# TensorE's instructions held in the order in which a two-layer hybrid backbone kernel gives them out

## The chip, the cores and the metric

The kernel runs on one core of a Trainium2 chip. The metric is device time in microseconds (us) of one execution. The chip's engines named here are TensorE (PE in the profile, with PEld for its weight loads), VectorE (DVE), ScalarE (ACT), GpSimd (POOL) and SyncE (SP, which here issues most of the DMAs).

## The reference, cut to what matters

Two post-norm layers run over 1024 latent tokens and 256 context tokens of width 1024, all in float32. In each layer the normalised input is modulated by vectors that come from a small product with `w_ada`, goes through one input projection, then through three branches (windowed attention, a gated depthwise convolution with LayerNorm, and a bidirectional linear recurrence), and the gated branches are merged and projected back.

```python
for l in range(DEPTH):                                    # DEPTH = 2, D_MODEL = 1024
    shift, scale, gate = jnp.split(jax.nn.silu(c) @ w_ada[l] + b_ada[l], 3, axis=-1)
    ...
    h = layer_norm(x) * (1.0 + scale[:, None]) + shift[:, None]
    hc = layer_norm(ctx) * (1.0 + scale_c) + shift_c
    q, k, v, g_att, u_conv, g_conv, x_lru, g_lru = split_in_proj(h @ w_in[l])
    ...
    y_att = window_attention(q, k, v, kc, vc, attn_sink[l])
    y_conv = conformer_conv(u_conv, ...)
    y_lru = hf_l + hb_l                                   # two rglru_direction scans
    out = merge_branches(h, (y_att, y_conv, y_lru), (g_att, g_conv, g_lru), ...)   # also uses sigmoid(h @ w_gate)
    x_new = deepnorm_post(x, gate[:, None] * out, ln_g[l], ln_b[l])
    # the context tokens go the same way, but not in the last layer
```

## The kernel before, in words

Every large product is made of float32r matmuls: the left and the right factor are each cut into a high part (`hi`) and a rest (`lo`), and hi·hi, hi·lo and lo·hi are added up in PSUM. So a weight arrives by DMA as `raw`, ACT copies it to `whi`, and DVE subtracts to get `wlo` (class `Wt`, method `load`; the tags `whi` and `wlo` have four buffers each, `NW = 4`). The activations stand transposed in SBUF as `hchi`/`hclo` (context, 256 columns) and `hlhi`/`hllo` (latent, two tiles of 512 columns).

The order of the work is made twice. First the Python code gives instructions out in an order of its own. In `phase1` (projections, branches, gates) and `phase2` (merge and output) a `Driver` runs generators, called streams here: recurrence, attention scores, attention values, convolution, gates and others. A stream yields between pieces of its work, and the Driver picks the next piece by its own estimate of when each engine is free (`LEAD`, `SLACK`, `MARGIN`, `PRIO`). PE, ACT and DVE are reached through a `Meter`, which adds up these estimates, so that nearly every one of their instructions has line 73 in the profile. Second, the tile framework is opened with `schedule_with_timeline_sim=True`: its scheduler takes the instructions of all engines with their dependencies and orders each engine's list anew by a simulation of its own. What runs is this second order.

Four places matter below. `emit_h0` is the start: it loads the input, normalises it, transposes it on PE (`p0` tiles in PSUM, 80 transposes), and ACT (`hf0`, then a copy) and DVE make the hi and lo parts. `ada_pair` is called 16 times between the gate projections of a layer: it loads two `w_ada` pieces, runs 16 matmuls with `csr` into one PSUM tile and calls `ada_fin`, where ACT copies the row (`arow`) and two small matmuls with `sel` follow; there is no yield in it and no wait for the weights' readiness:

```python
        for k in range(KD):
            for v in range(2):
                pe.matmul(out=ps[0:4, 0:256], lhsT=csr[:, k, :], rhs=ws[k // 4][v][:, k % 4, :],
                          start=(k == 0 and v == 0), stop=(k == KD - 1 and v == 1))
        ada_fin(l, [jj, jj + 1], ps, 4, row)
```

`att_values` transposes the softmax rows `P` into a PSUM tile `pt`, ACT makes `ph` and DVE makes `pl` from it, and the matmuls into `yp` follow; between the transposes and these matmuls the stream yields. `norm` in `phase2` normalises the finished rows `xp`, transposes them (eight transposes into one of the two `ps2` buffers) and ACT modulates them (`hf`), which gives the next layer its `hl`/`hc` tiles.

Of the kernel before, what the change touches and what calls it, by code (L numbers as in the profile page):

```python
# [51 lines left out]
class Meter:  # L52


    def __init__(self, eng, cost):
        self.eng, self.cost, self.t = eng, cost, 0.0

    def __getattr__(self, name):
        f = getattr(self.eng, name)
        if name.startswith("dma"):  # L60
            return f

        def call(*a, **k):
            out = k.get("out", a[0] if a else None)
            src = k.get("in_", out) if name in ("reduce_max", "bn_stats") else out
            n = 1
            for v in src.shape[1:]:
                n *= v
            if len(a) == 2 and name == "tensor_copy":
                k = dict(k, in_=a[1])  # L70
                a = a[:1]
            self.t += self.cost(name, n, k)
            return f(*a, **k)  # L73

        return call

# [113 lines left out]
def kernel(  # L190
# [5 lines left out]
):  # L196
    nc = tc.nc
    pool, sp = nc.gpsimd, nc.sync
    pe, act, dve = Meter(nc.tensor, pe_cost), Meter(nc.scalar, act_cost), Meter(nc.vector, dve_cost)
    drv_ = Driver(pe, act, dve)  # L200

    K = ctx.enter_context(tc.tile_pool(name="const", bufs=1))
# [118 lines left out]
    class Wt:  # L321


        def __init__(self, src, a, b, home=None):
            self.own = home is None
            if self.own:
                wlive[0] += 1
            self.ap, self.ready = drv_.side(lambda: self.load(src, a, b, home or W))
# [1135 lines left out]
```

## Time and profile before

| | |
|---|---|
| median of 3 runs | 2307.94 us (2307.21 to 2312.17) |
| profiled execution | 2307.8 us, of which the span of instructions is 2306.0 us |
| mean clock granted to TensorE | 0.990 of full speed |
| busy share of the span | PE 98%, PEld 81%, DVE 73%, ACT 44%, POOL 4% |

The page gives each engine's busy time; the windows view gives it for a stretch, with the granted clock in the column PEclk. In the timeline a row is a run of like instructions with its start and length; matmuls overlap, so the distance between two starts, not the length of a row, is what a matmul costs in a dense stretch. An idle time ahead of an instruction stands in brackets, with the instruction whose end released it.

### The profile page before, as it was taken

The numbers are of one execution on the slowest core, as the hardware profiler recorded it, in microseconds if no ns is written. First come the engines' busy times: TensorE is split into PE (matmuls) and PEld (weight loads), VectorE is DVE, ScalarE is ACT, GpSimd is POOL, SyncE is SP. The second block draws the span as 40 slices with busy tenths as digits, with TensorE's granted clock in tenths as the row PEclk, the third lists the DMA queues.
The fourth block names the chain that finished last, engine by engine and source line by source line (L and its number), as shares of the span: only waits on it lengthen the run. The fifth ranks groups of instructions, "written<-read, shape, count | busy, mean of one in ns | idle before, by whom it ended". The sixth has DMA issues, their size and how long they took to land.

```text
span 2306.0 us, 29961 instructions
## 1 busy us (share of the span) xinstructions
PE 2249.3 (98%) x11344; PEld 1871.8 (81%) x11344; DVE 1678.9 (73%) x2453; ACT 1003.4 (44%) x1642; POOL 86.7 (4%) x140
## 2 busy tenths in 40 slices
PE   7999999999999999999999999999999999999998
PEld 2888888888888887888888788888888878778886
DVE  5579967868959875545678749869778787655667
ACT  4555563245444575422122644565344456542110
POOL 1000000000000111000001100000000011000002
PEclk8999999999999999999999999999999999999999
DMA  7223323433334232655562222233423334347532
GB/s 276 76 73 101 115 73 126 142 112 108 108 101 138 80 117 87 203 167 168 151 206 74 94 66 67 80 92 128 142 90 97 89 122 131 111 136 227 160 128 92
DMA packets 270946, 279.90 MB, mean 121 GB/s; under 512 B 19769, under 2 KB 199889, under 8 KB 270801
## 3 DMA queue, kind: packets, MB, share of 16 engines
q1 hardware_dynamic: 242288, 226.06, 31.4%
q10 hardware_dynamic: 28512, 51.92, 6.4%
q8 instruction: 89, 1.46, 0.3%
q14 instruction: 57, 0.46, 0.1%
HBM read 203.04 MB, written 74.88 MB: 121 GB/s over the span
## 4 chain that ended last, share of the span: by engine, by line
PE 88%; DVE 5%; ACT 2%; DMA 2%; issue 2%; SPq 0%; POOLq 0%; POOL 0%; ACTq 0%; DVEq 0%
PE ps L73 82%; PE yp L73 3%; PE pt L73 2%; PE pa L73 1%; DVE acc L73 1%; DMA raw<-in_w_ada_dram 1%; DVE P L73 1%; DVE pl L73 1%; DVE wlo L73 1%; DMA yst<-yd 1%; ACT whi L73 0%; DMA qd<-qd 0%; DVE xp L73 0%; PE p L73 0%; ACT hf L73 0%
## 5 line engine op out<-in xcount | busy, mean ns | idle before, releaser
L73 PE MATMUL ps<-hlhi,whi 128*128 128x512 f32 x1728 | 681.9, 395 | 2.2 <-DVE gs L73 1.0
L73 PE MATMUL ps<-hllo,whi 128*128 128x512 f32 x1728 | 678.4, 393 | 0.0
L73 PE MATMUL ps<-hlhi,wlo 128*128 128x512 f32 x1728 | 676.8, 392 | 0.0
L73 PEld LDWEIGHTS ps<-hlhi,wlo 128*128 128x128 f32 x1728 | 325.8, 189 | 67.5 <-issue 0.4
L73 PEld LDWEIGHTS ps<-hlhi,whi 128*128 128x128 f32 x1728 | 326.5, 189 | 66.5 <-DVE pl L73 2.2
L73 PEld LDWEIGHTS ps<-hllo,whi 128*128 128x128 f32 x1728 | 326.2, 189 | 62.7 <-issue 0.7
L73 DVE SCALAR_TENSOR_TENSOR acc<-u,cwt,acc 128x1296 f32<-128x1296 f32 (+1 forms) x240 | 342.3, 1426 | 2.2
L73 ACT ACTIVATE whi<-raw 128x1024 fp32r<-128x1024 f32 x180 | 190.0, 1058 | 334.1 <-PE ps L73 299.9
L73 DVE TENSOR_TENSOR wlo<-raw,whi 128x1024 fp32r<-128x1024 f32 x180 | 220.4, 1225 | 95.1 <-ACT whi L73 91.5
L73 PE MATMUL ps<-yy,whi 128*128 128x512 f32 (+1 forms) x960 | 271.6, 368 | 2.8 <-DVE m L73 2.8
L73 PEld LDWEIGHTS ps<-yy,whi 128*128 128x128 f32 x960 | 173.7, 188 | 33.5 <-DVE m L73 3.2
L73 PE MATMUL ps<-yy,wlo 128*128 128x512 f32 (+1 forms) x480 | 176.6, 368 | 0.0
L73 ACT ACTIVATE ph<-pt 128x512 fp32r<-128x512 f32 x160 | 93.9, 591 | 130.5 <-PE pt L73 125.1
L73 DVE TENSOR_TENSOR pl<-pt,ph 128x512 fp32r<-128x512 f32 x160 | 108.9, 685 | 50.8 <-ACT ph L73 49.4
L73 PE MATMUL ps<-hchi,whi 128*128 128x256 f32 x480 | 135.6, 283 | 1.3 <-ACT whi L73 0.5
L73 ACT ACTIVATE P<-P,nm 128x640 f32<-128x640 f32 (+1 forms) x128 | 101.9, 798 | 79.7 <-DVE nm L73 79.6
L73 PE MATMUL ps<-hchi,wlo 128*128 128x256 f32 x480 | 135.3, 282 | 1.0 <-DVE wlo L73 1.0
L73 PE MATMUL ps<-hclo,whi 128*128 128x256 f32 x480 | 134.6, 281 | 0.0
L73 DVE CUSTOM_DVE_ANT_0 P<-ps,m_mid,nsink 128x640 f32<-128x640 f32 (+1 forms) x112 | 93.0, 859 | 42.3 <-PE ps L73 40.8
L73 ACT ACTIVATE tg<-ps,drv 128x512 f32<-128x512 f32 (+1 forms) x120 | 76.4, 637 | 68.3 <-PE ps L73 67.7
L73 PEld LDWEIGHTS ps<-yy,wlo 128*128 128x128 f32 x480 | 90.5, 188 | 15.0
L73 PE MATMUL pt<-ident,P 128*128 128x128 f32 x640 | 97.2, 274 | 3.1 <-DVE pl L73 1.4
(205 smaller groups left out, 3396.1 us busy)
## 6 DMA issues: line engine op xcount, KB each, us to landing
raw<-in_w_in_dram SPq DMA_DIRECT2D x60, 512.0 KB
raw<-in_w_ada_dram SPq DMA_DIRECT2D x48, 512.0 KB
raw<-in_w_gate_dram SPq DMA_DIRECT2D x48, 512.0 KB
th<-tg ACTq DMA_DIRECT2D x96, 256.0 KB
thl<-th SPq DMA_DIRECT2D x96, 256.0 KB
yd<-gs ACTq DMA_DIRECT2D x48, 256.0 KB
yst<-yd SPq DMA_DIRECT2D x48, 256.0 KB
raw<-in_w_branch_dram SPq DMA_DIRECT2D x24, 512.0 KB
```

The lines of the kernel that those rows point to most:

```text
L73: return f(*a, **k)
```

## The change

`Meter` gets a third argument, and PE's Meter is given `tc.keep_in_program_order`. That call links an instruction to the one that the code gave out before it on the same engine, by an edge that orders the two and makes no semaphore wait. The scheduler therefore has to leave PE's list as the code gave it out. ACT, DVE, POOL and SP are still ordered by the scheduler. No instruction is added or removed.

```diff
-    def __init__(self, eng, cost):
-        self.eng, self.cost, self.t = eng, cost, 0.0
+    def __init__(self, eng, cost, keep=None):
+        self.eng, self.cost, self.t, self.keep = eng, cost, 0.0, keep
...
             self.t += self.cost(name, n, k)
-            return f(*a, **k)
+            r = f(*a, **k)
+            return self.keep(r) if self.keep else r
...
-    pe, act, dve = Meter(nc.tensor, pe_cost), Meter(nc.scalar, act_cost), Meter(nc.vector, dve_cost)
+    pe, act, dve = Meter(nc.tensor, pe_cost, tc.keep_in_program_order), Meter(nc.scalar, act_cost), Meter(nc.vector, dve_cost)
```

**The start.** PE's list at the end of `emit_h0` before: `p0` are the transposed input tiles, `ps_808` and `ps_869` projections of layer 0.

```order
L73 MATMUL p0_613<-ident_81,x0_542 128x128
L73 MATMUL ps_808<-hllo_189,whi_699 128x512
L73 MATMUL ps_808<-hlhi_188,wlo_700 128x512
...
L73 MATMUL p0_622<-ident_81,x0_542 128x128
L73 MATMUL ps_869<-hlhi_190,whi_699 128x512
L73 MATMUL ps_869<-hllo_191,whi_699 128x512
...
L73 MATMUL p0_631<-ident_81,x0_542 128x128
L73 MATMUL ps_869<-hllo_191,whi_699 128x512
```

And after the change: the last transposes, then the first projection, `ps2_728`, whose PSUM banks are those that the `p0` tiles held.

```order
L73 MATMUL p0_622<-ident_81,x0_542 128x128
L73 MATMUL p0_631<-ident_81,x0_529 128x128
L73 MATMUL p0_631<-ident_81,x0_555 128x128
L73 MATMUL p0_631<-ident_81,x0_444 128x128
L73 MATMUL p0_631<-ident_81,x0_542 128x128
L73 MATMUL ps2_728<-hchi_184,whi_687 128x256
L73 MATMUL ps2_728<-hclo_185,whi_687 128x256
```

All 80 transposes now stand ahead of the first projection matmul; before, projections stood between them. The same holds where layer 0 passes into layer 1: the last six `ps2<-ident,xp` groups of `norm` now stand in one block ahead of layer 1's first projection, where before projections of layer 1 stood between them.

**An ada pair.** `ps_1420` is the pair's PSUM tile, `whi_1410` and `whi_1416` its two weights, `ps_1355` the gate projection ahead of it, which is the last to read `whi_1109` and `wlo_1110`. Before, PE's list at the second weight's first matmul and at the `sel` matmuls:

```order
L73 MATMUL ps_1469<-hllo_191,whi_1156 128x512
L73 MATMUL ps_1420<-whi_1416,csr_161 4x256
L73 MATMUL ps_1469<-hlhi_190,wlo_1157 128x512
...
L73 MATMUL ps2_1529<-hllo_189,whi_1054 128x512
L73 MATMUL ps_1420<-sel_162,arow_1407 128x2 x2
L73 MATMUL ps2_1529<-hlhi_188,wlo_1055 128x512
```

After:

```order
L73 MATMUL ps_1355<-hllo_191,whi_1109 128x512
L73 MATMUL ps_1355<-hlhi_190,wlo_1110 128x512
L73 MATMUL ps_1420<-whi_1410,csr_161 4x256
...
L73 MATMUL ps_1420<-wlo_1411,csr_161 4x256
L73 MATMUL ps_1420<-whi_1416,csr_161 4x256
...
L73 MATMUL ps_1420<-wlo_1417,csr_161 4x256
L73 MATMUL ps_1420<-sel_162,arow_1407 128x2 x2
```

Before, 19 other matmuls stood between the first weight's eight and the second weight's first, and 27 rows of other work between the last `csr` matmul and `sel`. Now all 16 stand together, and the `sel` matmuls right behind the last.

**An attention block.** Before, around the `pt` whose transposes stand between two values matmuls (`ps_5316` is a projection):

```order
L73 MATMUL yp_5173<-ph_5249,vs_3793 128x512
L73 MATMUL pt_5285<-ident_81,P_4660 128x128 x2
L73 MATMUL pt_5285<-ident_81,P_4744 128x128 x2
L73 MATMUL yp_5173<-pl_5250,vs_3793 128x512
L73 MATMUL yp_5173<-ph_5290,vs_3793 128x512
L73 MATMUL ps_5316<-hlhi_188,whi_5017 128x512
```

After:

```order
L73 MATMUL pt_5285<-ident_81,P_4744 128x128 x2
L73 MATMUL ps_5257<-hchi_184,whi_5017 128x256
...
L73 MATMUL ps_5257<-hchi_184,wlo_5018 128x256
L73 MATMUL ps_5316<-hlhi_188,whi_5017 128x512
...
L73 MATMUL ps_5316<-hlhi_188,wlo_5018 128x512
L73 MATMUL yp_5173<-ph_5249,vs_3793 128x512
```

Before, one matmul stood between `pt_5285` and `yp_5173<-ph_5290`, which reads what ACT makes of `pt_5285`. Now 24 projection matmuls stand behind the transposes, ahead even of the values of the block before.

## Rows read from the trace of the kernel before

**Rows 1.** The page: busy time by engine, and the chain that ended last.
```profile
PE 2249.3 (98%) x11344; PEld 1871.8 (81%) x11344; DVE 1678.9 (73%) x2453; ACT 1003.4 (44%) x1642; POOL 86.7 (4%) x140
...
PE 88%; DVE 5%; ACT 2%; DMA 2%; issue 2%; SPq 0%; POOLq 0%; POOL 0%; ACTq 0%; DVEq 0%
```

**Rows 2.** Windows view of four stages: length, busy time by engine, PEclk, DMA share.
```profile
57.00:70.00 13.00, 13.00 (x95) 12.04 (x94) 9.00 (x16) 13.00 (x20) 0.63 (x4) 0.98 0.32 97
100.00:450.00 350.00, 349.19 (x1881) 296.15 (x1880) 291.67 (x307) 170.20 (x217) 1.79 (x14) 1.00 0.33 104
450.00:950.00 500.00, 485.17 (x2718) 412.52 (x2717) 367.33 (x621) 257.21 (x504) 24.28 (x24) 0.99 0.36 111
1850.00:2100.00 250.00, 238.90 (x1155) 195.64 (x1154) 176.38 (x299) 134.93 (x245) 16.84 (x14) 0.99 0.42 134
```

**Rows 3.** Timeline of PE in attention: start, length, instruction, idle before and releaser.
```profile
590.66 0.60 PE L73 MATMUL pt<-ident,P 128*128 128x128 f32 x4
...
593.78 0.79 PE L73 MATMUL yp<-ph,vs 128*128 128x512 f32 x1 [2.29 <-ACT ph L73]
...
914.76 0.79 PE L73 MATMUL yp<-ph,vs 128*128 128x512 f32 x1 [2.39 <-DVE pl L73]
...
1974.41 1.01 PE L73 MATMUL ps<-ks,qh 128*128 128x384 f32 x2 [2.46 <-ACT qh L73]
```

**Rows 4.** Windows view of three short stretches around such idle times.
```profile
593.50:597.00 3.50, 3.22 (x8) 2.54 (x9) 3.43 (x6) 1.20 (x4) 0.00 (x0) 0.51 0.51 148
...
1029.00:1033.00 4.00, 1.54 (x10) 1.21 (x9) 1.95 (x4) 0.63 (x1) 0.00 (x0) 1.00 0.48 157
...
1310.00:1317.00 7.00, 4.47 (x15) 3.90 (x16) 4.58 (x9) 6.70 (x19) 1.13 (x5) 0.52 0.19 76
```

**Rows 5.** The page's costliest groups: the four that make hi and lo parts.
```profile
L73 ACT ACTIVATE whi<-raw 128x1024 fp32r<-128x1024 f32 x180 | 190.0, 1058 | 334.1 <-PE ps L73 299.9
L73 DVE TENSOR_TENSOR wlo<-raw,whi 128x1024 fp32r<-128x1024 f32 x180 | 220.4, 1225 | 95.1 <-ACT whi L73 91.5
...
L73 ACT ACTIVATE ph<-pt 128x512 fp32r<-128x512 f32 x160 | 93.9, 591 | 130.5 <-PE pt L73 125.1
L73 DVE TENSOR_TENSOR pl<-pt,ph 128x512 fp32r<-128x512 f32 x160 | 108.9, 685 | 50.8 <-ACT ph L73 49.4
```

**Rows 6.** Timeline of PE around the first ada pair.
```profile
95.03 0.39 PE L73 MATMUL ps<-hlhi,whi 128*128 128x512 f32 x1
95.26 0.39 PE L73 MATMUL ps<-hllo,whi 128*128 128x512 f32 x1
...
98.76 0.28 PE L73 MATMUL ps<-whi,csr 128*4 128x256 f32 x1
98.88 0.28 PE L73 MATMUL ps<-wlo,csr 128*4 128x256 f32 x1
...
104.81 0.60 PE L73 MATMUL ps<-sel,arow 4*128 4x2 f32 x4
```

**Rows 7.** Timeline of ACT at the start, at the pair and where the layers meet.
```profile
69.24 0.76 ACT L73 ACTIVATE hf<-p,ada 128x512 f32<-128x512 f32 x1
...
100.22 0.35 ACT L73 ACTIVATE arow<-ps 4x256 f32<-4x256 f32 x1
...
109.74 0.69 ACT L73 ACTIVATE A<-ps,drv 128x512 f32<-128x512 f32 x1
...
1319.18 2.90 ACT L73 ACTIVATE hf<-ps,ada 128x128 f32<-128x128 f32 x8 [0.30 <-DVE hllo L73]
```

**Rows 8.** Groups of PE from 55.2 to 70 us: count, busy time, mean ns.
```profile
L73 PE MATMUL ps<-hchi,whi 128*128 128x256 f32 x16 | 4.9, 309 | 0.0
...
L73 PE MATMUL ps<-hlhi,whi 128*128 128x512 f32 x7 | 2.8, 406 | 0.0
```

**Rows 9.** Groups of PE from 1303.5 to 1322.5 us.
```profile
L73 PE MATMUL ps<-ident,xp 128*128 128x128 f32 x28 | 4.7, 319 | 4.8 <-ACT hf L73 4.8
L73 PE MATMUL ps<-hlhi,whi 128*128 128x512 f32 x9 | 4.3, 495 | 0.0
...
L73 PE MATMUL ps<-hchi,whi 128*128 128x256 f32 x8 | 2.3, 288 | 0.0
```

## The prediction

> **What bounds the kernel now.** I read the page first. TensorE is busy 98% of the span, and the chain that ended last is 88% PE, 5% DVE and 2% ACT [rows 1]. So PE is the bound, and a change of its order can only matter where PE waits: it gains where an idle time goes, and it loses, nearly one for one, where a new one comes. The windows by stage then show where PE waits today. From 100 to 450 us it is idle for 0.8 of 350 us at full clock; that stage has nothing to give. From 450 to 950 us, where attention of layer 0 runs, it is idle for 500 - 485.2 = 14.8 us, and from 1850 to 2100 us, attention of layer 1, for 250 - 238.9 = 11.1 us, both at a clock of 0.99 [rows 2]. The timeline of PE shows what these idle times are: 2.3 to 2.5 us each, behind `ph`, `pl` or `qh`, when PE has too little other work between the transposes into `pt` (590.66) and the matmul that reads `ph` (593.78) [rows 3]. `ph` and `pl` take 0.59 and 0.69 us by themselves [rows 5]; the rest is queueing on ACT and DVE. After such a wait the clock can fall: 593.5 to 597 us ran at 0.51, that is at 1.2 instead of 2.4 GHz [rows 4].
>
> A matmul of 512 columns costs 0.23 us in a dense stretch (95.03 to 95.26) and one of 256 columns 0.12 us (98.76 to 98.88) [rows 6]. I count the orders of before and after in these units.
>
> **What can be gained.** The pool is 14.8 + 11.1 us of idle time, and for the clock 1% of 750 us = 7.5 us, up to 11 with the rounding of 0.99: 33 to 37 us [rows 2]. Of the 160 steps from `pt` to the matmul that reads its `ph`, 49 have less than 3 us of PE work between them before, and 25 after. The block in the section on the change is such a step: the 24 projection matmuls behind `pt_5285` are 12 x 0.12 + 12 x 0.23 = 4.2 us, more than the 3.1 us from 590.66 to 593.78 [rows 3]. But 18 of the 25 lie at the end of attention of layer 1, where no projections are left and where the given order is tighter than the scheduler's was. I leave some 8 us of the pool there and take a gain of 25 us; the bounds are 5 us (the waits move to other places in attention) and 37 us (all goes).
>
> **What is lost.** Five terms, in the order of the program.
>
> 1. The start. Before, PE did 48 projection matmuls of 256 columns and 19 of 512 between the transposes up to 70 us (16 and 7 of the first kind in the rows, the other kinds alike) [rows 8]. They were free, because ACT was the bound there, busy 13.0 of 13.0 us [rows 2]. They are 48 x 0.12 + 19 x 0.23 = 10.1 us, and they now come after all transposes. The first of them needs the `p0` banks, so it waits for the last `hf`, some 70.0 (69.24 + 0.76) to 71.7 us if one more `hf` must end first [rows 7]. 10.1 + 1.7 = 12 us; bounds 8 (ACT gets through sooner, with PE never late) and 16 (PE comes to it with a low clock).
>
> 2. Where the layers meet. The six groups of transposes need two `ps2` buffers in turn, each set free by eight `hf` of 2.9 us; the fourth of these sets ends at 1319.18 + 2.90 = 1322.1 us [rows 7], and only behind it can the last group and the first projection of layer 1 run. Before, 24 matmuls of 256 columns and 27 of 512 had been done by 1322.5 us (8 and 9 of the first kind) [rows 9]: 2.9 + 6.2 = 9.1 us. With something for the clock, which fell to 0.52 there even before [rows 4], 10.5 us; bounds 7 and 13.
>
> 3. `sel` behind `csr`. In the first pair the last `csr` matmul began at 98.88, `arow` at 100.22 for 0.35 us, and `sel` at 104.81, which hid it [rows 6, 7]. Now `sel` is next on PE: with the same `arow` PE stands from 99.0 to 100.6, 1.6 us. In that pair ACT was still at a `whi` of 1.06 us. With ACT free the floor is the length of the last matmul's row, 0.28, plus 0.35, less 0.12: 0.5 us [rows 6, 7]; behind a `whi` just begun it is over 1.6 us. I take 1.0 us, 16 times: 16 us, bounds 8 and 26.
>
> 4. The second weight of a pair. `whi_1416` takes the buffer that `whi_1109` held. Now `whi_1109` is read last just ahead of the pair, and only eight `csr` matmuls, 0.94 us, lie between. In that time ACT must make `whi` (1.06 us) and DVE `wlo` (1.22 us) one after the other [rows 5], 2.3 us: a stall of at least 1.4 us. With an evacuation of 0.69 us ahead on ACT [rows 7] and a like one on DVE it is nearer 3 us. I count six pairs with just this distance, at 2.2 us, and five with 1.4 to 3.2 us of PE work in between, at 1 us: 18 us, bounds 8 and 28. Before, 19 other matmuls lay there, and the stage of 100 to 450 us had no idle time at all [rows 2].
>
> 5. PSUM. Without the scheduler's choice PE comes in some ten places within 0.7 us to a bank whose evacuation takes 0.69 us (the `A` of 109.74) [rows 7]. 4 us, bounds 0 and 12.
>
> Edits that cost nothing: the edges themselves, as no wait or instruction is added. DMA issues hang on SP, ACT and POOL, whose lists move little; a weight's load starts when its buffer is free, which is priced in term 4.
>
> Losses 12 + 10.5 + 16 + 18 + 4 = 60.5 us, less 25 us: 35.5 us. The profiled execution took 2307.8 us (span 2306.0 and 1.8 around it), 0.1 us below the median, so the forecast is 2343 us. Its own range, with the terms' errors taken as independent, is 2322 to 2362 us.
>
> **The rivals.**
>
> *Faster, all at the floors.* If ACT and DVE, which the scheduler still orders freely, take `arow`, `whi` and `wlo` at once, the losses are 8 + 7 + 8 + 8 + 0 = 31 us, and if attention loses all its idle time and low clock the gain is 37: 2302 us, 0.26% faster. It decides where terms 3 and 4 together stay under some 17 us. For it: ACT is busy only 44% of the span [rows 1], 49% from 100 to 450 us [rows 2]. Against it: DVE is busy 83% of that stage [rows 2], so a `wlo` seldom finds it free. 15% for this and other ways to be faster.
>
> *No change.* Gain and loss meet within 0.2% (4.6 us, about what a measurement of this kernel can tell from nothing), for instance 35 us each: 2308 us. That the edges would not bind is ruled out by the order itself. 8%.
>
> *Slower still, by the clock.* Each pair would have two idle times of 1 to 3 us a few us apart. After 2.3 us of idle at 591 us the clock fell for 3.4 us, which cost 1.7 us; at 1310 us it fell for 6.8 us, which cost 3.4 us; but the 2.5 us of idle time between 1029 and 1033 us left it at 1.00 [rows 3, 4]. If eleven pairs (those of term 4) bring it down once, that is 19 to 37 us on top, less what the terms already hold: some 2368 us, 2360 to 2385. The stage of the pairs is otherwise dense, which speaks against it. 22%. The Trainium skill, "TensorE: Matmul & The Clock Gate", section "HAM oscillation — how this bites in real kernels", tells of a kernel in which bursts of matmuls are parted by waits, and each burst begins with a cold array anew. [...]
>
> **How the numbers follow.** 55% for the forecast, 22% for the clock, 8% for no change, 15% for faster: slower 77%, same 8%, faster 15%. The range leaves out the far ends: below 2298 us, where the faster rival would need more than the pool, and above 2385 us.
>
> **What would show it.** Start: no `hchi` or `hlhi` matmul before 70 us, and the first at 70 to 72. Layers: six groups `ps2<-ident,xp` in a row with waits behind `hf`, the first projection of layer 1 some 20 us after the first of them. Pairs: an idle time of 0.5 to 2 us ahead of each `sel`, released by ACT `arow`, and of 1.4 to 3 us ahead of a `csr` matmul, released by `whi` or `wlo`, where the stage from 100 to 450 us had none. Attention: idle time from 450 to 950 us well under 14.8 us once the pairs' own waits are taken off, the wait at `yp_5173<-ph_5290` gone, and the tail of layer 1 no better than before. I would be wrong if the pairs' waits came out at 0.5 us, if attention still waited as much in other places, or if the clock fell at most pairs.

## The result: 4.9% slower, about three times the loss that was forecast

| | before | after |
|---|---|---|
| median | 2310.06 us (2307.21 to 2312.89, 4 runs) | 2423.45 us (2418.34 to 2428.88, 4 runs) |
| ratio | 1 | 1.049, 95% interval 1.0472 to 1.0507 |
| span of the profiled execution, clock | 2306.0 us, 0.990 | 2419.0 us, 0.974 |

The forecast was 2343 us, with a range of 2298 to 2385. The direction was right; the time lies outside the range. The page of the changed kernel, busy time by engine and the chain that ended last, answers to [rows 1]:

```profile
PE 2288.2 (95%) x11344; PEld 1896.0 (78%) x11344; DVE 1682.7 (70%) x2453; ACT 1012.8 (42%) x1642; POOL 86.4 (4%) x140
...
PE 79%; DVE 10%; ACT 5%; issue 3%; DMA 3%; SPq 0%; POOL 0%; ACTq 0%; POOLq 0%; DVEq 0%
```

The same 11344 matmuls keep PE busy for 2288.2 instead of 2249.3 us, 38.9 us more, and PE is idle for 2419.0 - 2288.2 = 130.8 instead of 56.7 us, 74.1 us more. Together these are the 113 us. The matmuls are the same, so the longer busy time has to come from how they ran. Summed over the stretches with a granted clock of 0.50, PE is busy for 90.8 us in the change and for 30.1 us before; half of the 60.7 us between them, 30 us, is what the lower clock adds. The other 9 us go with the number of waits, 99 against 49: ahead of a wait the last matmul counts with its whole row, for instance 0.28 us where it costs 0.12 us in a dense stretch, and 50 x 0.16 = 8 us is an estimate of that. The waits view of PE sums its idle time by what ended it; its columns are the sum, how often, and the longest. After the change:

```profile
PE ps L73 <- ACT arow L73: 19.3, 16, 5.7
PE ps L73 <- ACT hf L73: 16.7, 5, 4.1
PE ps L73 <- DVE wlo L73: 11.6, 10, 2.6
PE ps L73 <- ACT xh L73: 10.5, 3, 7.2
PE ps L73 <- DVE ql L73: 7.1, 10, 2.1
PE yp L73 <- DVE pl L73: 6.5, 14, 1.0
PE ps L73 <- DVE xl L73: 6.0, 4, 2.5
```

and before:

```profile
PE yp L73 <- ACT ph L73: 9.1, 9, 2.3
...
PE ps L73 <- ACT hf L73: 4.8, 2, 3.9
...
PE ps L73 <- DVE wlo L73: 1.0, 2, 0.8
...
PE ps L73 <- ACT arow L73: 0.2, 1, 0.2
```

The waits for `ph` are fewer, and in their place stand `arow`, `hf`, `wlo`, and `xh` and `xl` of the recurrence gates, which had not stood in the list at all. To see where in the program the time went, I cut PE's timeline at the starts of nine instructions that both kernels have. Before they lie at 95.5, 447.4, 932.6, 1021.2, 1233.3, 1652.0, 2061.4, 2078.4 and 2296.5 us, after at 108.4, 493.8, 989.8, 1083.1, 1293.1, 1746.5, 2169.9, 2192.0 and 2409.5 us. The table gives each stage's length before, and how much longer it is in the change and in the runs told below (each from its own profiled execution; executions of one kernel lie up to some 10 us apart, so a few us between two runs tell little).

| stage ends at | before | after | ada_free | ends_free | gates_free | att_free | att_only | proj_only | filler_free | proj_filler |
|---|---|---|---|---|---|---|---|---|---|---|
| first `csr` of a pair | 95.5 | +12.9 | +15.9 | -1.5 | +11.8 | +12.8 | +0.5 | +1.5 | +7.5 | -0.1 |
| first scores, layer 0 | 351.9 | +33.5 | +18.0 | +34.6 | +33.0 | +35.7 | -0.1 | +23.1 | +22.0 | -0.9 |
| last values, layer 0 | 485.2 | +10.8 | +10.7 | +13.7 | +6.7 | -2.4 | +7.3 | -5.7 | +18.4 | +1.1 |
| first `yy`, phase 2 | 88.6 | +4.8 | +4.8 | +5.0 | +4.8 | +4.8 | +0.2 | +4.8 | +0.2 | 0.0 |
| first `xp` transpose | 212.2 | -2.2 | -2.5 | +3.6 | +1.1 | -1.1 | +0.1 | -0.9 | +1.0 | -0.3 |
| first scores, layer 1 | 418.6 | +34.8 | +36.5 | +27.5 | +22.9 | +39.4 | +0.1 | +18.9 | +23.2 | +1.2 |
| last values, layer 1 | 409.5 | +14.0 | +12.6 | +16.8 | +12.6 | +2.1 | +8.3 | -0.7 | +8.0 | -0.8 |
| first `yy`, phase 2 | 17.0 | +5.1 | +5.1 | +5.1 | +5.1 | 0.0 | -0.2 | 0.0 | +5.1 | 0.0 |
| last matmul | 218.1 | -0.6 | -0.6 | -0.6 | -0.6 | +0.1 | +1.8 | +0.5 | -0.6 | 0.0 |

The windows view of three of these stages before, and of two after:

```profile
95.50:447.40 351.90, 351.09 (x1888) 297.02 (x1887) 293.44 (x306) 172.11 (x218) 1.79 (x14) 1.00 0.33 104
932.60:1021.20 88.60, 88.60 (x462) 76.29 (x461) 38.26 (x62) 29.16 (x51) 0.30 (x3) 1.00 0.58 189
1233.30:1652.00 418.70, 412.70 (x1942) 345.06 (x1941) 330.94 (x372) 213.60 (x307) 16.76 (x38) 0.99 0.29 94
```

```profile
989.80:1083.10 93.30, 93.30 (x482) 80.20 (x481) 39.02 (x63) 30.75 (x54) 0.30 (x3) 1.00 0.59 190
1293.10:1746.50 453.40, 421.57 (x1940) 349.31 (x1938) 333.14 (x379) 213.01 (x307) 18.68 (x39) 0.96 0.26 86
```

A stage also gets longer when matmuls move into it. The stages up to the first `yy` have no idle time before or after; the one of layer 0 has 482 matmuls instead of 462, and 20 x 0.23 = 4.6 us. So its +4.8 us, and the +5.1 us of layer 1 in the same way, are work that moved there and no loss of their own.

Two stages, mostly of projections, where PE was idle for 0.8 and 6.0 us before, lose 68 of the 113 us. The two stages of attention, from which 25 us were to come, lose 25 us. In the first of them PE is idle for 496.0 - 470.7 = 25.3 us. Nine ada pairs lie there and make 10.9 us of it (9.0 us behind `arow`), and 14.4 us are left, where there had been 14.8. In the second the idle time rises from 10.8 to 20.3 us.

What the steps of the forecast said can be read in PE's timeline of the changed kernel: the start, the third ada pair, the wait of a pair that was far longer than the others, the transposes where the layers meet, and a recurrence gate.

```profile
74.29 0.58 PE L73 MATMUL ps<-hchi,whi 128*128 128x256 f32 x1 [4.07 <-ACT hf L73]
...
230.61 0.28 PE L73 MATMUL ps<-wlo,csr 128*4 128x256 f32 x1 [0.98 <-DVE wlo L73]
...
232.04 0.60 PE L73 MATMUL ps<-sel,arow 4*128 4x2 f32 x4 [0.46 <-ACT arow L73]
...
271.11 1.01 PE L73 MATMUL ps<-sel,arow 4*128 4x2 f32 x4 [5.72 <-ACT arow L73]
...
1370.58 1.97 PE L73 MATMUL ps<-ident,xp 128*128 128x128 f32 x8 [4.00 <-ACT hf L73]
1375.54 1.97 PE L73 MATMUL ps<-ident,xp 128*128 128x128 f32 x8 [2.99 <-ACT hf L73]
...
1503.85 0.59 PE L73 MATMUL ps<-xh,lwh 128*128 128x260 f32 x1 [7.17 <-ACT xh L73]
1506.94 0.58 PE L73 MATMUL ps<-xl,lwh 128*128 128x260 f32 x1 [2.51 <-DVE xl L73]
```

The first projection comes behind `hf`, as foretold, at 74.29 us; the pairs wait for `wlo` and for `arow`; the `xp` groups wait for `hf` one after another. The gate at 1503.85 stands in no step of the forecast. For the windows view, the same stretches' answer to [rows 2, 4]: the stage from the first pair to the first scores, attention of layer 0, 3.4 us behind the pair at 228 us, 4 us behind an earlier pair with like waits, and the place where the layers meet.

```profile
108.40:493.80 385.40, 364.20 (x1881) 307.19 (x1880) 298.57 (x310) 174.85 (x219) 1.81 (x14) 0.96 0.30 96
493.80:989.80 496.00, 470.71 (x2635) 399.56 (x2635) 360.48 (x611) 252.27 (x488) 21.73 (x21) 0.99 0.33 103
...
233.20:236.60 3.40, 3.40 (x10) 2.66 (x9) 3.40 (x5) 1.06 (x1) 0.00 (x0) 0.50 0.61 188
...
172.00:176.00 4.00, 4.00 (x22) 3.53 (x23) 4.00 (x5) 1.39 (x2) 0.00 (x0) 1.00 0.41 120
...
1366.00:1387.00 21.00, 8.34 (x39) 6.90 (x38) 13.82 (x26) 19.42 (x45) 2.91 (x10) 0.59 0.26 81
```

The stage from the first pair to the first scores ran at 1.00 before and now at 0.96. Its 33.5 us are 20.4 us of idle time (21.2 against 0.8) and 13.1 us of longer busy time (364.2 against 351.1). Where the layers meet, ACT is busy for 19.4 of 21 us and PE for 8.3.

### The profile page after: what moved, and what is told of

The parts are those of the page before. It is cut to its first block, busy times and chain, and to the rows that moved or that the text cites. A ratio compares the mean times of both kernels' runs of the same rounds, so it can differ in the third digit from the quotient of the medians.

```text
span 2419.0 us, 29971 instructions
## 1 busy us (share of the span) xinstructions
PE 2288.2 (95%) x11344; PEld 1896.0 (78%) x11344; DVE 1682.7 (70%) x2453; ACT 1012.8 (42%) x1642; POOL 86.4 (4%) x140
## 4 chain that ended last, share of the span: by engine, by line
PE 79%; DVE 10%; ACT 5%; issue 3%; DMA 3%; SPq 0%; POOL 0%; ACTq 0%; POOLq 0%; DVEq 0%
PE ps L73 73%; PE yp L73 2%; PE pt L73 2%; DVE acc L73 2%; DVE wlo L73 1%; PE pa L73 1%; ACT whi L73 1%; DVE xc L73 1%; ACT hf L73 1%; DMA raw<-in_w_in_dram 1%; DVE pl L73 1%; ACT P L73 1%; DMA thl<-th 1%; DVE gs L73 0%; DVE st L73 0%
## 5 line engine op out<-in xcount | busy, mean ns | idle before, releaser
L73 PE MATMUL ps<-hlhi,whi 128*128 128x512 f32 x1728 | 690.2, 399 | 1.5 <-DVE gs L73 1.5
L73 PE MATMUL ps<-hchi,whi 128*128 128x256 f32 x480 | 143.5, 299 | 5.8 <-ACT hf L73 4.1
L73 PE MATMUL ps<-hclo,whi 128*128 128x256 f32 x480 | 139.8, 291 | 0.0
L73 PEld LDWEIGHTS ps<-hchi,whi 128*128 128x128 f32 x480 | 96.1, 200 | 10.1 <-ACT hf L73 4.3
```

Of the source, the lines that this page charges most:

```text
L73: r = f(*a, **k)
```

## The experiments

In these kernels the edge is made by a few lines of their own. It goes to the last instruction that was held, and not to the one given out just before, so that a freed instruction is not held between its neighbours. With the switch on everywhere this gives PE's list of the change.

```python
class Pin:
    def __init__(self, tc, on=True):
        self.tc, self.on, self.last = tc, on, None
    def __call__(self, r):
        if self.on:
            if self.last is not None:
                self.tc.add_manual_dep(r.ins, self.last.name, ...)   # NoSync: order alone
            self.last = r.ins
        return r
```

Shares are given as points of the time before (1% is 23.1 us), since each ratio has its own runs of the kernel before beside it; the change is at 1.049.

**One stream freed at a time.** Each frees one group of matmuls, all others stay in the given order.

```diff
+        pin.on = False                     # ada_free: in ada_pair, around the csr matmuls and ada_fin
         for k in range(KD):
             for v in range(2):
                 pe.matmul(out=ps[0:4, 0:256], lhsT=csr[:, k, :], rhs=ws[k // 4][v][:, k % 4, :],
...
         ada_fin(l, [jj, jj + 1], ps, 4, row)
+        pin.on = True
```

> The matmuls of ada_pair (csr and sel) are left to the scheduler, all other PE instructions keep the given order. Theory A (each wait at a pinned place costs its idle time and then the low clock behind it): after the change PE waited 19.3 us for arow and 12.6 us for wlo and whi, and the clock was low for 41 us right behind eight pairs, which is 20 us lost; so about 52 us come back, 2371 us. Theory B (idle time alone, the clock would fall anyhow): 32 us come back, 2391 us. Theory C (the pairs are not where the time goes; the lists of ACT and DVE, which the scheduler also made anew, are): under 10 us come back, 2413 us or more.

Measured 2404.93 us, ratio 1.0406 (1.039 to 1.0423): 0.84 points or 19 us come back, against 52, 32 and under 10 expected. None of the three numbers holds. The table shows where: the stage of the first seven pairs still loses 18.0 of 33.5 us, and PE's largest waits in that stage are now for weights of the projections with `w_in` (3.75 us for a `whi` at 263.99 us, 3.62 us for its `wlo` at 270.19 us).

```diff
-    pin = Pin(tc, True)
+    pin = Pin(tc, False)                   # ends_free: held only from the first ada pair on
...
     def ada_pair(l, jj, row):
+        pin.on = True
...
+                pin.on = False             # and in norm
                 for kk in range(KD):
                     pe.transpose(ps[:, kk * 128:kk * 128 + 128], xt[:, kk * 128:kk * 128 + 128], ident)
+                pin.on = True
```

> PE keeps the given order only from the first ada pair on, and norm's transposes where the layers meet are left to the scheduler. Theory A: the first csr matmul comes 13 us earlier again, at 95 to 97 us, and the 14 us of idle time behind hf where the layers meet, with 20 us of low clock, mostly go: some 13 + 18 us come back, 2392 us. Theory C: the start comes back alone, 2410 us.

Measured 2409.78 us, 1.0415 (1.0392 to 1.0438): 0.75 points, 17 us: the number of Theory C. The start comes back in full (+12.9 to -1.5 us). Where the layers meet little does. The freed transposes also move the cut in the table, so the stages on both sides of it have to be taken together: they lose 31.1 instead of 32.6 us, though PE's waits for `hf` there fall from 12.7 to 8.4 us.

```diff
+                            pin.on = False     # gates_free: the recurrence gates
                             for j, (a, r) in enumerate(((lwh, "xh"), (lwh, "xl"), (lwl, "xh"))):
                                 pe.matmul(out=ps[:, 0:n], lhsT=a[:, wo:wo + 128], rhs=v[r, dr][:, o:o + n], ...)
+                            pin.on = True
```

> The matmuls of the recurrence gates (lwh, lwl by xh, xl) are left to the scheduler. My prediction had no term for them. Theory A: after the change PE waited 10.5 us for xh, 6.0 us for xl and 4.5 us for A and I, and the clock fell behind two of these waits, 14 us at half; 21 + 7 us come back, 2395 us. Theory C: under 10 us.

Measured 2411.38 us, 1.0429 (1.0406 to 1.0453): 0.61 points, 14 us, most of it where the layers meet (the two stages there lose 24.0 instead of 32.6 us).

For attention the switch stands around the matmuls of the scores, the transposes of `P` and the matmuls of the values: off there and on elsewhere in att_free, the reverse in att_only.

> The changed kernel with only the attention matmuls (scores, transposes of P, values) left to the scheduler. Theory D (the given order of attention costs 16 us by itself, as in the run with only attention pinned): 2407 us or less, all of it won between the first scores and the last values matmul of each layer. If attention's waits come from the other streams' order: 2418 to 2430 us.

Measured 2396.59 us, 1.0362 (1.0343 to 1.0381): 1.28 points, 30 us, nearly all in attention's own two stages and the step into phase 2 of layer 1 (part of that is matmuls that moved to other stages).

> The reverse: only the attention matmuls (scores, transposes of P, values) keep the given order among themselves; all other PE instructions are left to the scheduler. My prediction took a gain of 25 us from attention: 2285 us. Theory D (the given order removes the waits for ph but puts others for ql, qh and pl in their place, 24.7 us against 22.7 us before): no gain, 2305 to 2315 us.

Measured 2323.98 us, 1.0057 (1.0038 to 1.0076). Attention held alone makes the kernel slower by 13 us. Theory D was nearer, and still too kind: held alone, the given order is no gain there.

**All three engines in the given order.** ACT's and DVE's Meters get such a switch too.

> PE's list as in the changed kernel, and ACT's and DVE's instructions (not their DMA issues) also held in the given order. Theory E (PE waits because its given order meets lists of ACT and DVE that the scheduler made by other rules, for instance wlo queued behind 1.5 us steps of the convolution): with all three from one plan the waits for wlo, ql and arow shrink, 2340 to 2390 us. Theory F (the given order itself is too tight, since the plan's estimates are short of what ACT and DVE really take): no better than the change, 2415 us or more, and up to 2500 where three lists now stand in line for each other.

Measured 2787.38 us, 1.2064 (1.2042 to 1.2085), with the clock at 0.92. The waits view of this kernel begins:

```profile
PE ps L73 <- DVE wlo L73: 103.0, 46, 7.8
PE ps L73 <- ACT whi L73: 96.3, 31, 14.8
PE ps L73 <- ACT xp L73: 71.2, 7, 13.0
```

That is 400 us above the range of Theory E, and 290 us above even the 2500 us of Theory F. The waits for `wlo` are nine times those of the change, so the lists that the scheduler made for ACT and DVE had softened the change. As holding ACT and DVE brings waits of its own, this run doesn't tell how many of the 113 us come from a held list that meets free ones.

**Is it DVE's queue?** In the gate at 1503.85 the `xh` of ACT had waited 5.21 us for `xc` of DVE, and steps of the convolution stood between those of `xc`. So I took most of these steps away, in the kernel before and in the changed one.

```diff
-                    dve.scalar_tensor_tensor(out=acc[:, QA:QE], ...)
+                    if k < 7:
+                        dve.scalar_tensor_tensor(out=acc[:, QA:QE], ...)
+                    else:
+                        dve.t += dve_cost("scalar_tensor_tensor", QE - QA, dict(in0=u, scalar=tap(k)))
```

> The kernel before with the depthwise convolution cut from 31 taps to 7 (24 of 31 DVE steps of 1.4 us per channel group left out, 192 in all, some 270 us of DVE's work; the Driver's clock counts them still, so that the code gives out the same order). PE's own work is the same. It only has the waits of attention and of the ends to lose: 2285 to 2308 us. It is the base for the next run.

> The changed kernel with the same taps left out; PE's list is the same, instruction for instruction. Theory H (the change made PE's waits as long as DVE's queue: xc, wlo, xl, ql and pl stand behind steps of the convolution, and with an idle DVE they come in time): the distance to the run without the edges falls from 113 to 35 to 60 us, what is left being arow, hf and the start. Theory I (the given order leaves too little room even for an idle DVE): the distance stays at 90 us or more.

Measured 2301.9 us, 0.9958 (0.9942 to 0.9973), and 2399.56 us, 1.0384 (1.0365 to 1.0404). The distance is still 97.7 us. So these steps in DVE's queue explain some 15 us, mainly at the gates (the waits for `xh` where the layers meet fall from 10.5 to 3.7 us), and Theory I's number holds for the rest. DVE is still busy for 60% of the span, so what an idle DVE would leave is not shown.

**Work put into the pairs' waits.**

```diff
+            if k == 3:
+                for i in range(8):        # zr is zero: adds nothing to the sum
+                    pin(nc.tensor.matmul(out=ps[0:4, 0:256], lhsT=zr, rhs=ws[0][0][:, i % 4, :], ...))
+        for i in range(4):
+            pin(nc.tensor.matmul(out=ps[0:4, 256:512], lhsT=csr[:, 0, :], rhs=ws[1][0][:, i % 4, :], ...))
         ada_fin(l, [jj, jj + 1], ps, 4, row)
```

> The changed kernel with twelve matmuls more in each ada pair that are not needed: eight with a left factor of zeros between the first and the second weight, and four of the pair's own into an unused part of its PSUM tile ahead of sel, so that PE works where it had waited. They are 12 x 0.12 = 1.4 us, 22 us for 16 pairs where nothing hides them. Theory A with the clock as a cost: the clock stays up behind the pairs, 41 us at half become 10 or less, 15 us come back, and with 5 to 10 us of matmuls that no wait hides the time is some 2415 us, with a clock of 0.98 or more. If the clock doesn't matter or falls all the same: 2428 to 2440 us.

Measured 2424.8 us, 1.0492 (1.0475 to 1.0509), the time of the change, though PE has 192 matmuls, some 22 us, more to do. From 108 to 789 us, where the pairs lie, the windows view shows for the change and for this run:

```profile
108.40:789.00 680.60, 645.15 (x3465) 545.28 (x3463) 513.99 (x668) 310.20 (x487) 2.02 (x17) 0.97 0.32 101
```

```profile
108.30:789.00 680.70, 657.67 (x3657) 552.63 (x3655) 518.40 (x673) 311.95 (x489) 2.01 (x17) 0.99 0.33 102
```

PE's idle time falls from 35.5 to 23.0 us, by 12.4 us. Its busy time rises by 12.5 us (657.7 less 645.2) for some 22 us of added work, so the clock, which rises from 0.97 to 0.99, gives back about 10 us. So the added work was paid for by idle time and clock in about equal parts. The clock fell because PE stood still in the pairs, and that is a cost of its own; my number for this run was 10 us too hopeful.

**Held only in the middle.**

```diff
+                pin.on = l == 0            # in att_scores; off again behind phase 2 of layer 0
```

> Only from the first scores of layer 0 to the end of its phase 2, and there not for ada pairs, recurrence gates, attention, the convolution's two LayerNorm products and norm's transposes, PE keeps the given order; elsewhere the scheduler is free. In the run with the projections pinned this stretch was 5.7 us shorter than before from the first scores to the last values, and 0.9 us in phase 2. If that is the order's own merit: 2302 to 2306 us, faster than before. If it was only work moved out of the stretch: 2309 to 2320 us.

Measured 2320.07 us, 1.0036 (1.0024 to 1.0047): slower. The shorter stage in proj_only was work moved out of it: by the windows view it has 2609 matmuls, before 2639, and 30 x 0.23 = 7 us.

**Who fills the gaps.** proj_only frees the pairs, the gates, attention, the ends, and holds mainly the projections, the small transposes and phase 2.

> Ada pairs, recurrence gates, attention, norm's transposes and all before the first ada pair are left to the scheduler; what keeps the given order is mainly the projections, the small transposes and phase 2. If what the single edits brought back adds up (18 for the pairs, 13 for the ends, 12 for the gates, and 16 by which attention alone was slower), the time is 2423 - 59 = 2364 us. Theory A (streams wait for one another only through the pinned places; with these free little is left): 2310 to 2330 us. Theory G (any projection pinned in the given order waits for its weight, whatever else is free): 2360 us or more, with wlo and whi as the first releasers.

Measured 2349.81 us, 1.0165 (1.0149 to 1.0181): 3.25 points come back, 75 us. The four single releases sum to 0.84 + 0.75 + 0.61 + 1.28 = 3.48 points. So they nearly add up (the 2364 us of the expectation had used 16 us for attention instead of 30). 1.65 points, 38 us, are left. PE's timeline of this run has the largest wait of what is left:

```profile
252.37 0.41 PE L73 MATMUL ps<-hclo,whi 128*128 128x256 f32 x1
260.41 0.58 PE L73 MATMUL ps<-hchi,wlo 128*128 128x256 f32 x1 [7.63 <-DVE wlo L73]
```

PE's list at that place (`ps_2254` is a projection with `w_in`, `ps2_2242` one of the gates stream, whose weight `whi_1937` and PSUM tile had been in use since 25 rows further up):

```
L73 MATMUL ps_2254<-hclo_185,whi_2207 128x256
L73 MATMUL ps_2254<-hchi_184,wlo_2208 128x256 [waits DVE_49]
L73 MATMUL ps_2254<-hchi_184,whi_2207 128x256
L73 MATMUL ps_2254<-hclo_185,whi_2207 128x256
L73 MATMUL ps_2254<-hchi_184,wlo_2208 128x256
L73 MATMUL ps2_2242<-hchi_184,whi_1937 128x256
```

PE stood for 7.6 us at a matmul that lacked its `wlo`. DVE made this `wlo` at 259.14 us, though its `whi` was there at 251.94 us: in DVE's list a scan of 2.34 us and steps of `xc` (1.55 us) and of the convolution (1.55 us), among others, stood ahead of it. Four rows behind the matmul at which PE stood were the gates stream's matmuls, which lacked nothing. The next two runs free these (filler_free as shown; in proj_filler a counter in `Pin` does the same).

```diff
             ti, t0, n = nt
+            filler = wide                  # gemm_nt is called with wide=True by the gates stream alone
...
+                    pin.on = not filler
                     pe.matmul(out=ps[:, 0:n], lhsT=w[a][:, k, :], rhs=r[b][:, k, :], ...)
+                    pin.on = True
```

> The changed kernel with only the projections of the gates stream (w_gate, the work that nothing in phase 1 waits for) left to the scheduler, which may put them into any gap of the rest. Theory J (the pinned order lacks only work to put into its gaps, and one free stream is enough): the losses of the two stages of recurrence and ada pairs, 33.5 and 34.8 us, shrink to 10 to 15 us each, 2375 to 2385 us. Theory A (each pinned place costs by itself, as the single edits suggest by adding up): 2410 us or more.

Measured 2391.01 us, 1.0354 (1.0336 to 1.0372): 1.36 points, 31 us, about what freeing attention brought (30 us) and more than the other three, but not the 40 to 50 us of Theory J. The two stages fall to +22.0 and +23.2.

> The run with mainly projections pinned (2350 us), with the gates stream's projections free as well. Theory J: the 23 and 19 us that this run still loses in the two stages go to under 8 us each, 2316 to 2330 us. Theory G (the other projections wait for their own weights all the same): 2340 us or more.

Measured 2312.17 us, 1.0012 (1.0002 to 1.0021). All but 3 us come back, with the other projections and phase 2 still in the given order. The waits view of proj_only from 95 to 480 us, and of proj_filler from 95 to 447 us:

```profile
PE ps L73 <- DVE wlo L73: 12.4, 5, 7.6
PE ps L73 <- ACT arow L73: 3.0, 3, 1.3
PE ps L73 <- ACT whi L73: 2.1, 1, 2.1
```

```profile
PE ps L73 <- ACT tg L73: 0.9, 2, 0.5
PE ps L73 <- DVE wlo L73: 0.3, 1, 0.3
```

The waits for `wlo` are gone though the projections that had them are still held among themselves. In PE's list of proj_filler 24 matmuls of 512 columns of the gates stream (`ps2_2443`) stand between the pair's `sel` and the same `ps_2254<-hchi_184,wlo_2208`, 24 x 0.23 = 5.5 us of work, where proj_only has none of them. Theory J holds for this remainder: the scheduler had hidden these waits by moving the gates stream.

That the gates stream is a filler and not a stream that was late itself can be read for the whole kernel, when PE's list is laid beside the timeline. In the change and in proj_only no matmul of the gates stream waits for its `whi` or `wlo`; its longest waits are 4.07 us (the first projection, at 74.29 us) and 3.14 us (where the layers meet), both for `hf`. In proj_only 14.2 of the 16.2 us of waits for `whi` and `wlo` stand ahead of projections with `w_in`.

What proj_filler still holds asks for little by itself. Before the change the scheduler had left the projections with `w_in` and phase 2 nearly in the given order: 217 of these 6048 matmuls would have to move to give it. With the 2880 of the gates stream, which are in order among themselves but for two, it is 692 of 8928. What the scheduler had changed was mostly how the streams stand between one another.

## Why the prediction was wrong, step by step

- **What bounds the kernel** was right: PE is the bound, and time moves with its waits and its clock.
- **The gain of 25 us from attention** is the step that failed most. The block that I showed behaved as foretold: there is no wait at `yp_5173<-ph_5290` any more, and the waits behind `ph` fell from 9.1 us in 9 cases to 3.0 in 6. But I had counted only the distance from `pt` to the matmul that reads `ph`. In their place PE waits for the split of `q` (for `ql` 7.1 us instead of 0.9) and for `pl` at `yp` (6.5 us instead of 3.1). That the given list leaves less room ahead of `ql` is likely, but no count here shows it. Instead of a gain of 25 us the two stages have a loss of 25 us, 14 of them without the pairs' waits. Held alone, attention costs 13 us (att_only); inside the change, freeing it returns 30 us (att_free).
- **The start** (term 1, 12 us): 12.9 us later at the first pair, and all of it back in ends_free. The cause was right, the size partly by luck: the first projection comes at 74.3 and not at 70 to 72 us, the clock is at half up to 79.6 us, and against both, 353 instead of 364 matmuls lie ahead of the first pair.
- **Where the layers meet** (term 2, 10.5 us): the cause was right. Of the 16.7 us behind `hf` in the list above, 4.1 are those at the start; the rest is in this stage, whose waits view is:

```profile
PE ps L73 <- ACT hf L73: 12.7, 4, 4.0
PE ps L73 <- ACT xh L73: 10.5, 3, 7.2
PE ps L73 <- DVE xl L73: 4.8, 3, 2.5
PE ps L73 <- ACT A L73: 3.1, 4, 0.9
PE ps L73 <- ACT I L73: 0.7, 1, 0.7
```

  Before, it was 4.8 us behind `hf` and 1.2 us behind `pj`. So the transposes add 7.9 us of idle time, the recurrence gates 19.1 us (`xh`, `xl`, `A` and `I`), and longer busy time 8.9 us (421.6 against 412.7).
- **sel behind csr** (term 3, 16 us): 19.3 us in 16 waits. Near in sum, in part by luck: seven of them were 0.46 us, near the floor, and one was 5.72 us.
- **The second weight** (term 4, 18 us): 10.8 us in nine pairs, all behind `wlo`; the rest of the 12.6 us for `wlo` and `whi` is one projection with `w_in`. The mechanism was right, the size too large. In the pair at 168 us ACT made `whi` from 168.16 and DVE `wlo` from 169.25 us, one right behind the other, and PE waited 0.98 us, as in three more pairs. My least of 1.4 us compares with what PE loses from start to start: there two steps from 169.00 to 170.53 us took 1.53 us instead of 0.24, a loss of 1.3 us. Terms 3 and 4 are 30 us of idle time, but freeing the pairs brings back only 19 us: with the pairs out of the way PE came to the next held projection sooner and waited there.
- **PSUM** (term 5, 4 us): waits for `A` and `I`, evacuations of the recurrence gates, are 3.1 and 1.4 us, in six places. Right.
- **Missing**: the recurrence gates. `xh` and `xl` cost 16.5 us of idle time where there had been no row; gates_free returns 14 us. I had looked for close distances in the pairs and in attention and not in every stream.
- **The clock** stood at 22% as a rival, with 19 to 37 us on top. It came, with some 30 us: the granted clock fell at or right behind seven of the 16 pairs, and also at the start, where the layers meet and behind two waits of the recurrence gates. In the pairs' stretch the fill run gives about 10 us of it back. How much of the rest is lost time, and how much lay under ACT-bound stretches as at 1366 us, stays open. In the kernel that the Trainium skill tells of in the section cited there ("TensorE: Matmul & The Clock Gate", "HAM oscillation — how this bites in real kernels") the waits between bursts are some 3 to 5 us, for DMA. The waits of the pairs are shorter but for one, and the clock fell behind some of them all the same, at 0.98 and 0.46 us for instance, and not behind others.

In idle time the five terms come to 7.9 + 7.9 + 19.1 + 10.8 + 4.5 = 50 us (the start, `hf`, `arow`, `wlo`, `A` and `I`, each less what was there before), where the forecast had 60.5 us with some clock in it. The recurrence gates add 16.5 us. Of the 74 us of idle time 7 are left for attention and the rest, where the forecast had a credit of 25 us. The longer busy time, 39 us, stood in it only as a rival and at the margins of two terms. So what failed was a credit that did not exist, one stream that I had not costed, and the clock that I had put into a rival. Behind much of this lies one thing that the forecast did not see as a mechanism: before, the scheduler could put the gates projections, which nothing in phase 1 waits for, into any gap. In the given order a stream stops PE where it is late and can't be used to fill another's gap.

What stays open: freeing the gates stream alone returns 31 us, freeing it after the four other groups returns 35 us more than those. No run frees another stream of like size in its place and holds the gates stream. So it isn't shown that the filler has to be the stream without deadlines; it may be that enough free work of any kind would do.

## What to carry to other kernels

Before an engine's order is held, count for every stream, not only for the one with visible stalls, how much other work lies between each instruction and the one that feeds it; a distance shorter than the feeding chain can become a stall of the whole engine. Then look for the stream that nothing waits for: it is what a scheduler can put into the gaps. Here, leaving it free brought back 31 of 113 us by itself, and all but 3 us together with the four groups whose distances were short. And price the clock: two waits of 1.4 us together were followed by 3.4 us at half clock, 1.7 us more, at one pair and by nothing at another.

## What the runs showed of the hardware

The clock behind short waits was not the same each time. The pairs at 168 and 228 us had the same two waits, 0.98 us for `wlo` and 0.46 us for `arow`; behind the first PE stayed at 1.00 (172 to 176 us), behind the second it ran at 0.50 for 3.4 us (233.2 to 236.6 us). Where the layers meet it stayed at half for 20.5 us:

```profile
1369.80:1390.30 20.50, 11.06 (x46) 9.70 (x47) 10.44 (x19) 19.59 (x47) 2.36 (x9) 0.50 0.18 58
```

The longest wait for `arow`, 5.72 us, was only in part ACT being busy. ACT's timeline of the changed kernel ahead of it:

```profile
264.55 1.06 ACT L73 ACTIVATE whi<-raw 128x1024 fp32r<-128x1024 f32 x1 [0.48 <-DVE wlo L73]
268.43 1.06 ACT L73 ACTIVATE whi<-raw 128x1024 fp32r<-128x1024 f32 x1 [2.82 <-DMA raw<-in_w_in_dram]
269.40 1.26 ACT L73 ACTIVATE kh<-pj 64x512 fp32r<-64x512 f32 x2
270.69 0.37 ACT L73 ACTIVATE arow<-ps 4x256 f32<-4x256 f32 x1
```

PE's last `csr` matmul ended at 265.39 us. ACT then stood 2.82 us for the DMA of a later weight, with `arow` two rows behind it in its list, while PE stood for `arow`. With PE's order held, a wait of ACT for something else became a wait of PE.
